# Hybrid decoder block: the retention norm on GpSimd and ScalarE, and four more gate blocks by seven products

## The chip, the cores and the metric

The kernel runs on one core of one Trainium2 chip. The metric is the device time of one execution in microseconds (us), taken as the median of several runs. PE is TensorE (matmuls), PEld its weight loads, DVE is VectorE, ACT is ScalarE, POOL is GpSimd, and SP is the engine that issues most DMAs.

## The reference, cut to what matters

One layer, batch 1, 1024 positions, width 1024, all float32. The part that the change touches is the retention branch of the token mixer, its gate, and the modulation vector:

```python
mod = jax.nn.silu(c) @ w_ada[l] + b_ada[l]            # 6 x 1024: sh1, sc1, g1, sh2, sc2, g2
h = modulate(rms_norm(x, norm1_g[l]), sh1, sc1)
rq, rk, rv, rg = parts[0], parts[1], parts[2], parts[3]   # parts of h @ w_in
ro = retention(rq, rk, heads(rv, RET_HEADS))          # 4 heads, dk 256, dv 512, chunks of 128
mu = jnp.mean(ro, axis=-1, keepdims=True)
var = jnp.mean(jnp.square(ro - mu), axis=-1, keepdims=True)
ro = (ro - mu) * lax.rsqrt(var + GN_EPS)
ro = ro * gn_g + gn_b
ret_out = (jax.nn.silu(rg) * ro) @ w_ret_out
```

In a chunk: `s = (q k^T) * decay`, `o = s v + (q state) * q_decay`, `state = state * decay^128 + (k * k_decay)^T v`. The rest of the block (dilated window attention, merge by gates, squared-ReLU MLP, norms) is not touched.

## The kernel before

**Precision.** Every float32 matmul is made of three passes: each operand is split into a high part (a copy in the reduced matmul format) and a low part (the rest), and `mm3` adds low x high, high x low and high x high (lines 207, 209, 211). A weight split (`split_w`) is a ScalarE copy (line 197) and a VectorE subtraction (line 198).

**Direct blocks and pairs.** A block is 128 output columns for all 1024 positions. A direct block (`proj_mm`) takes 8 k tiles x 3 passes x 2 halves of 512 positions = 48 matmuls. Two blocks can instead be made together as a pair by a seven-product scheme for 2 x 2 block matrices (class `Blocks`): 7 products x 4 k tiles x 3 passes = 84 matmuls, with sums of weight quarters and of results on VectorE beside them. A pair of kind "s" holds Silu gate blocks of retention; its result goes to DRAM (`srg_d`) and comes back in the head that needs it.

**Stages and their times in the profile.** The first values and operand sums; 22 pairs (`queries_keys`, 180 to 597 us); the values of retention (`values`, 597 to 712 us, ten groups of four); retention (712 to 981 us, `chunk`, 4 heads x 8 chunks); then attention, merge and MLP.

**Modulation rows.** From the 17th pair on `mod_turn` is called after every product of a pair and after every value group's part. It loads one row of `w_ada` (512 KB) with SP into one of two buffers (`cs`, shown as cossin), and two rows later the buffer is used by a VectorE multiply-accumulate (line 1252) before it is loaded again (line 1254). 32 rows are taken so.

**A retention chunk.** The order is written out by hand, and every engine issues in that order. In chunk (h, c), with g = 8 h + c: two `kv` products (state update); some units of the gate (`rg_mm(n)`, one unit is one k tile, six matmuls); the VectorE state update (line 745), its ScalarE high part (749) and VectorE low part (750); `ahead(2)`, which splits the weights of the next step; `s_kt(g + 1)`, which makes the scores sT and the transposed key kT of the next chunk, and from them `sm`, `smh`, `sml`, `kh`, `kl`; the output `o`; `jit_qk` for two chunks ahead (ScalarE copy, GpSimd low part, line 617); the transposes oT of the last chunk's normed output with their ScalarE copies; one more gate unit; the norm. The norm is bn_stats, bn_aggr and a small step on VectorE (772 to 774), a power on GpSimd (775), a small product (776) and the 512-wide `onm` (778) on VectorE. In the first four chunks of heads 1 to 3 `u_final` follows for the head before: a ScalarE scale and shift (688), the VectorE product with the gate (690), and the DMA of `y`.

**Gate units.** Each head has four gate blocks: three are direct, 8 units each, and three units stand in each chunk (`RG`); the fourth comes from a pair.

**PSUM.** PSUM has eight banks. During retention four are one-bank tiles with tag "s" (sT, kT, kv, o, oT in rotation) and four are two two-bank tiles with tag "mm" (the gate).

Of the kernel before, what the change touches and what calls it, by code (L numbers as in the profile page):

```python
# [40 lines left out]
CS_QD = 132  # L41
CS_QD2 = 136
# [98 lines left out]
def block_kernel(ctx, tc, io, stop=None, dbg=None):  # L141
# [12 lines left out]
    def banks(single):  # L154
# [11 lines left out]
    def ps_mm(name):  # L166
        return PS["p"].tile([P, 2, 512], F32, tag="mm", bufs=2, name=name)

# [343 lines left out]
    def etile(name, dt=F32):  # L512
        return R["p"].tile([P, 1024], dt, tag="E", bufs=12, name=name)
# [116 lines left out]
    def s_kt(i):  # L630

        p = R["p"]
        g = i
        h, c = divmod(g, NC)
        t = hd["j", g]
        ps = ps_s(f"sT{h}{c}")
        for i in range(2):
            nc.tensor.matmul(ps[:, :2 * C], t[:, 0, 2 + i, :], t[:, :, i, :], start=i == 0, stop=False,
                             skip_group_check=True)
            nc.tensor.matmul(ps[:, :C], t[:, 1, 2 + i, :], t[:, 0, i, :], start=False, stop=i == 1,  # L640
                             skip_group_check=True)
        pk = ps_s(f"kT{h}{c}", (P, 2, P)) if c < NC - 1 else None
        if pk is not None:
            for i in range(2):
                nc.tensor.transpose(pk[:, i, :], hd["qk", g][:, 2 + i], ident)
# [7 lines left out]
        nc.vector.tensor_add(sm, sm, ps[:, C:2 * C])  # L653
        nc.vector.tensor_mul(sm, sm, decay[:, h * C:(h + 1) * C])
        hd["s", g] = (smh, sml)
        if pk is not None:
            kd = ct[:, CS_KDEC + h:CS_KDEC + h + 1]
            if g == 0:
                kh, kl = R["kh"], R["kl"]
            else:  # L660
                kh = p.tile([P, 2, P], F32R, tag="kh", bufs=1, name=f"kh{h}{c}")
                kl = p.tile([P, 2, P], F32R, tag="kl", bufs=1, name=f"kl{h}{c}")
            nc.scalar.mul(kh, pk, kd)
        nc.scalar.copy(smh, sm)
        if pk is not None:
            nc.vector.scalar_tensor_tensor(flat(kl), flat(pk), kd, fv(flat(kh)), op0=ALU.mult, op1=ALU.subtract)
            hd["k", g] = (kh, kl)
        nc.vector.tensor_sub(sml, sm, fv(smh))

    def on_T(h, c):  # L670

        po = ps_s(f"oT{h}{c}", (P, 4, P))
        on = hd["o", h, c]
        if c == 0:
            hd["on", h] = [etile(f"on{h}{e}") for e in range(4)]
        for e in range(4):
            nc.tensor.transpose(po[:, e, :], on[:, e * P:(e + 1) * P], ident)
        for e in range(4):
            nc.scalar.copy(hd["on", h][e][:, c * C:(c + 1) * C], po[:, e, :])

    def u_final(h, es=range(4), queue=nc.sync):
        for e in es:
            i = h * 4 + e
            t = hd["on", h][e]
            for hf in range(2):
                neg = 16 if hf == i % 2 else 0
                b = t[:, 512 * hf:512 * hf + 512]
                nc.scalar.activation(b, b, AF.Identity, scale=gnv[0][:, neg + i:neg + i + 1],
                                     bias=gnv[1][:, neg + i:neg + i + 1])
            nc.vector.tensor_mul(t, t, hd["srg", h, e])  # L690
            queue.dma_start(y_d[h][:, 2 * (i % 2):2 * (i % 2) + 2, e // 2], t.rearrange("p (t x) -> p t x", t=2))
# [12 lines left out]

    def rg_out(h, c):

        if "rgs" in hd:
            e = {1: 0, 2: 0, 4: 1, 5: 1, 7: 2}[c]
            hd["srg", h, e] = etile(f"srg{h}{e}")
            nc.scalar.activation(hd["srg", h, e], flat(hd.pop("rgs")), AF.Silu)  # L710
        if c == 6:
            hd["srg", h, 3] = etile(f"srg{h}3")
            nc.sync.dma_start(hd["srg", h, 3], srg_d[h])

    def chunk(h, c, ahead, w=None):
# [21 lines left out]
        rg_mm(1 if g == 0 else RG[h][c] - 1)  # L737
# [9 lines left out]
        if g > 0:  # L747
            for i in range(len(kvs)):
                nc.scalar.copy(sh1[:, i, :], st[:, i, :])  # L749
                nc.vector.tensor_sub(sl1[:, i, :], st[:, i, :], fv(sh1[:, i, :]))  # L750
        if g == 0:
            jit_qk(2)
        ahead(2)
        if 0 < g < NG - 1:
            s_kt(g + 1)
# [15 lines left out]
        gr = p.tile([P, 1], F32, tag="gr", bufs=2, name=f"gr{h}{c}")  # L771
        nc.vector.bn_stats(bn, po)
        nc.vector.bn_aggr(ba, bn)
        nc.vector.tensor_scalar(gr, ba[:, 1:2], ct[:, CS_QD2 + h:CS_QD2 + h + 1], GN_EPS, op0=ALU.mult, op1=ALU.add)
        nc.gpsimd.tensor_tensor(gr, gr, mhalf[:, 0:1], op=ALU.pow)
        nc.vector.tensor_mul(gr, gr, ct[:, CS_QD + h:CS_QD + h + 1])
        on = p.tile([P, DV], F32, tag="on", bufs=1, name=f"onm{h}{c}")
        nc.vector.tensor_scalar(on, po, ba[:, 0:1], gr, op0=ALU.subtract, op1=ALU.mult)
        hd["o", h, c] = on
        rg_out(h, c)  # L780
        if h > 0 and c < 4:
            u_final(h - 1, (c,))
# [8 lines left out]
    srg_d = [dram.tile([P, S], F32, name=f"srgd{h}") for h in range(H)]  # L791
# [333 lines left out]
    def sums_of_h(name, ms=range(4)):  # L1125

        for m in ms:
# [18 lines left out]
            if name != "t4":  # L1146
# [10 lines left out]
    s_pairs = [("s", i) for i in range(H // 2)]  # L1157
    PAIRS = [{"r": r_pairs, "a": a_pairs, "g": g_pairs, "k": k_pairs, "s": s_pairs}[i].pop(0)
             for i in "rargrarkrargrarkgagass"]
# [29 lines left out]
    def a_out(q, n, x, y=None):  # L1189
# [19 lines left out]
        if n in ("12", "21"):  # L1209
# [6 lines left out]
            elif pair[0] == "s":  # L1216
                dst = srg_d[2 * pair[1] + i]
# [166 lines left out]
    def values(ahead):  # L1384
# [43 lines left out]
        banks(False)  # L1428
# [4 lines left out]

    for h in range(H):
        for c in range(NC):
            steps.add((lambda h, c: lambda ahead, *w: chunk(h, c, ahead, *w))(h, c),
                      ([wsplit(io["w_rg"][3 * h + (0, 2, 5).index(c)])] if c in (0, 2, 5) else []),
# [393 lines left out]
    def att_step(pair, a):  # L1831

        def body(*args):
            ps = ps_mm(f"ak{pair}1{a}")
# [993 lines left out]
def _constants():  # L2828
# [9 lines left out]
    for h in range(H):  # L2838
# [4 lines left out]
        cst[:, CS_QD + h] = np.exp(lg * (i + 1))  # L2843
        cst[:, CS_QD2 + h] = np.exp(2 * lg * (i + 1))
# [19 lines left out]
def pack(x, c, w_ada, b_ada, norm1_g, w_in, rel_bias, ret_gn_g, ret_gn_b,  # L2864
# [17 lines left out]
        "w_rg": _cols(w[:, 4096:6144].reshape(1024, 4, 4, P)[:, :, :3].reshape(1024, 1536)),  # L2882
        "w_rg2": _pairs(w[:, 4096:6144].reshape(1024, 4, 4, P)[:, :, 3].reshape(1024, 512)),
# [33 lines left out]
```

## Time and profile before

| | |
|---|---|
| median of 3 runs | 2175.4 us (2174.5 to 2175.61) |
| profiled execution | 2173.28 us, its span 2171.3 us |
| TensorE | 2144.7 us busy (99%), 10036 matmuls, clock 0.999 |
| VectorE | 1520.4 us busy (70%) |
| ScalarE | 959.3 us busy (44%) |
| GpSimd | 165.7 us busy (8%) |
| HBM | 324.13 MB read, 160.32 MB written |

Matmuls overlap, so the time of one in the profile (0.39 us for 512 columns) is longer than the distance from one to the next. The end of an instruction on VectorE and ScalarE overlaps a little with the start of the next one, too; distances between starts tell what a step costs its engine.

### The profile page before, as it was taken

The numbers are of one execution on the slowest core, as the hardware profiler recorded it, in microseconds if no ns is written. First come the engines' busy times: TensorE is split into PE (matmuls) and PEld (weight loads), VectorE is DVE, ScalarE is ACT, GpSimd is POOL, SyncE is SP. The second block draws the span as 40 slices with busy tenths as digits, with TensorE's granted clock in tenths as the row PEclk, the third lists the DMA queues.
The fourth block names the chain that finished last, engine by engine and source line by source line (L and its number), as shares of the span: only waits on it lengthen the run. The fifth ranks groups of instructions, "written<-read, shape, count | busy, mean of one in ns | idle before, by whom it ended". The sixth has DMA issues, their size and how long they took to land. (4 is left out here: it accounts for less than half of the span.)

```text
span 2171.3 us, 27289 instructions
## 1 busy us (share of the span) xinstructions
PE 2144.7 (99%) x10036; PEld 1782.4 (82%) x10036; DVE 1520.4 (70%) x2358; ACT 959.3 (44%) x1757; POOL 165.7 (8%) x199
## 2 busy tenths in 40 slices
PE   8999999999999999999999999999999999999998
PEld 6888888888887788888888888888778888888887
DVE  6886777777656677776667644677876665877855
ACT  5543322323334455556656625434454455533413
POOL 0001111100001112211110000001000000000003
PEclk9999999999999999999999999999999999999999
DMA  9859998835588744436877366653144435645322
GB/s 383 282 208 309 285 306 265 243 117 194 186 301 303 234 148 151 160 127 197 218 194 196 115 245 211 217 191 132 64 175 160 150 136 193 253 135 173 109 88 78
DMA packets 162674, 425.18 MB, mean 196 GB/s; under 512 B 28005, under 2 KB 55916, under 8 KB 159468
## 3 DMA queue, kind: packets, MB, share of 16 engines
q1 hardware_dynamic: 150264, 374.90, 48.3%
q0 software_dynamic: 9584, 48.24, 9.9%
q8 instruction: 79, 1.29, 0.2%
q10 hardware_dynamic: 2692, 0.30, 0.1%
q14 instruction: 55, 0.45, 0.1%
HBM read 324.13 MB, written 160.32 MB: 223 GB/s over the span
## 5 line engine op out<-in xcount | busy, mean ns | idle before, releaser
L207 PE MATMUL qap<-hh,qaw 128*128 128x512 f32 x264 | 102.7, 389 | 0.0
L209 PE MATMUL qap<-hl,qaw 128*128 128x512 f32 x264 | 102.7, 389 | 0.0
L211 PE MATMUL qap<-hh,qaw 128*128 128x512 f32 x264 | 102.7, 389 | 0.0
L617 POOL TENSOR_TENSOR j<-qk,j 128x512 fp32r<-128x512 f32 x32 | 42.8, 1338 | 454.8 <-ACT j L616 454.8
L2235 POOL TENSOR_TENSOR accnf<-accnf,sqnf 128x256 f32<-128x256 f32 (+1 forms) x18 | 16.6, 922 | 609.6 <-ACT sqnf L2231 609.6
L2339 ACT ACTIVATE a<-a 128x512 f32<-128x512 f32 x48 | 30.3, 631 | 72.8 <-DVE a L2338 71.3
L749 ACT CAST stateh<-state 128x512 fp32r<-128x512 f32 x54 | 32.9, 622 | 57.8 <-DVE state L745 55.7
L209 PEld LDWEIGHTS qap<-hl,qaw 128*128 128x128 f32 x264 | 49.5, 188 | 10.4
L211 PEld LDWEIGHTS qap<-hh,qaw 128*128 128x128 f32 x264 | 49.6, 188 | 10.3
L207 PEld LDWEIGHTS qap<-hh,qaw 128*128 128x128 f32 x264 | 49.5, 188 | 10.2
L2547 ACT CAST w2h<-w2s 128x512 fp32r<-128x512 f32 x36 | 22.4, 621 | 80.3 <-DVE w2s L2585 80.3
L264 DVE TENSOR_TENSOR fw<-w1r,fw 128x512 fp32r<-128x512 f32 x48 | 32.9, 688 | 33.6 <-ACT fw L254 33.6
L264 DVE TENSOR_TENSOR qaw<-wa,qaw 128x512 fp32r<-128x512 f32 x66 | 44.0, 687 | 9.4 <-ACT qaw L254 9.4
L2070 DVE TENSOR_TENSOR rwl<-rwl,rwh 128x1024 fp32r<-128x1024 f32 x25 | 30.2, 1221 | 29.0 <-ACT rwh L2100 29.0
L207 PE MATMUL fp<-h2h,fw 128*128 128x512 f32 x128 | 50.0, 390 | 0.0
L209 PE MATMUL fp<-h2l,fw 128*128 128x512 f32 x128 | 49.8, 389 | 0.0
L211 PE MATMUL fp<-h2h,fw 128*128 128x512 f32 x128 | 49.8, 389 | 0.0
L207 PE MATMUL roa<-rh,rwl 128*128 128x512 f32 x128 | 49.8, 389 | 0.0
L209 PE MATMUL roa<-rl,rwh 128*128 128x512 f32 x128 | 49.8, 389 | 0.0
L211 PE MATMUL roa<-rh,rwh 128*128 128x512 f32 x128 | 49.8, 389 | 0.0
L1603 ACT ACTIVATE P<-P,ng 128x128 f32<-128x128 f32 (+1 forms) x96 | 41.9, 438 | 17.6 <-DVE ng L1595 17.5
L292 DVE TENSOR_TENSOR qat<-qat,qap 128x512 f32<-128x512 f32 x22 | 15.1, 688 | 42.8 <-PE qap L211 35.8
(3089 smaller groups left out, 7187.8 us busy)
## 6 DMA issues: line engine op xcount, KB each, us to landing
cossin<-in_w_ada_dram SPq DMA_DIRECT2D x32, 512.0 KB, 3.5
v<-vd SPq DMA_DIRECT2D x32, 512.0 KB, 4.3
w1r<-in_w_ff_dram SPq DMA_DIRECT2D x32, 512.0 KB, 4.6
yt<-y POOLq DMA_DIRECT2D x24, 512.0 KB, 7.5
xsd<-as SPq DMA_DIRECT2D x24, 512.0 KB, 3.1
w2r<-in_w_ff2s_dram SPq DMA_DIRECT2D x24, 512.0 KB, 6.4
em<-in_w_ada_dram SPq DMA_DIRECT2D x16, 512.0 KB, 10.2
wrvs<-in_w_rv_dram POOLq DMA_DIRECT2D x16, 512.0 KB, 9.8
```

What stands on the lines that cost most here:

```text
L207: nc.tensor.matmul(o, wl, xh, start=first, stop=False, skip_group_check=skip)
L209: nc.tensor.matmul(o, wh, xl, start=False, stop=False, skip_group_check=skip)
L211: nc.tensor.matmul(o, wh, xh, start=False, stop=last, skip_group_check=skip)
L264: nc.vector.tensor_sub(t[:, 512:], src, fv(t[:, :512]))
L292: nc.vector.tensor_sub(u, u, b)
L617: nc.gpsimd.tensor_sub(t[:, 1], src, fv(t[:, 0]))
L749: nc.scalar.copy(sh1[:, i, :], st[:, i, :])
L1603: nc.scalar.activation(v, v, AF.Exp, bias=ng[:, blk:blk + 1], accum_out=st[:, g, blk, 2 + a:3 + a])
L2070: nc.vector.tensor_sub(lo, fv(lo), fv(hi))
L2235: (nc.vector if f == 7 else nc.gpsimd).tensor_add(G["acc", key], G["acc", key], sq)
L2339: nc.scalar.activation(o, o, AF.Relu)
L2547: nc.scalar.copy(hi, src)
```

## The change

- The norm: the small step on VectorE becomes one addition, with the epsilon scaled for each position (`CS_EQ`). GpSimd makes minus the mean (a product with -1), the power, and their product. The 512-wide norm is a ScalarE activation with scale and bias from these, and leaves VectorE.
- The gate: two blocks of each head are direct, two come from pairs; there are four "s" pairs instead of two, 24 pairs in all. `RG` has 64 units instead of 96, spread unevenly. The Silu of a direct block is made in two halves.
- PSUM in retention: five one-bank tiles "s" and three one-bank tiles "rg". The banks change back at the first attention step.
- Weights of a gate block are tied to the step before the one that uses them. `ahead(2)` stands behind `s_kt`, and so does the second low part of the state (in the middle of `s_kt`'s VectorE steps).
- `u_final`: its ScalarE part stands ahead of the norm's activation, its product and DMA in the next chunk.
- Copies of oT: two of 256 columns instead of four of 128.
- Modulation rows: one in two turns instead of 7 in 16.

```diff
-CS_QD = 132
-CS_QD2 = 136
+CS_NEG = 132
+CS_EQ = 136
...
-        PS["n"] = 8 if single else 4
+        PS["n"] = 8 if single else 5 if ret else 4
...
+    def ps_rg(name):
+        return PS["p"].tile([P, 512], F32, tag="rg", bufs=3, name=name)
...
-        return R["p"].tile([P, 1024], dt, tag="E", bufs=12, name=name)
+        return R["p"].tile([P, 1024], dt, tag="E", bufs=4, name=name)
...
-    def s_kt(i):
+    def s_kt(i, mid=None):
...
             hd["k", g] = (kh, kl)
+        if mid:
+            mid()
         nc.vector.tensor_sub(sml, sm, fv(smh))
...
-        for e in range(4):
-            nc.scalar.copy(hd["on", h][e][:, c * C:(c + 1) * C], po[:, e, :])
+        for e in range(2):
+            nc.scalar.copy(hd["on2", h][e][:, :, c * C:(c + 1) * C], po[:, 2 * e:2 * e + 2, :])
...
-    RG = ((6, 2, 2, 3, 3, 3, 3, 2),) + ((3,) * NC,) * (H - 1)
+    RG = (6, 2, 2, 2, 1, 1, 2, 3), (2, 2, 2, 2, 2, 1, 1, 3), (2, 2, 2, 2, 2, 1, 1, 3), (3, 2, 2, 2, 2, 2, 2, 0)
...
-                hd["rgk"], hd["rgw"], hd["rgp"] = 0, hd["rgws"].pop(0), ps_mm("rg")
+                hd["rgk"], hd["rgw"], hd["rgp"] = 0, hd["rgws"].pop(0), [ps_rg(f"rg{i}") for i in range(2)]
...
-                hd["rgs"] = hd["rgp"]
+                i = hd["rgi"] = hd.get("rgi", -1) + 1
+                t = hd["srg", i // 2, i % 2] = etile(f"srg{i // 2}{i % 2}")
+                for j, ps in enumerate(hd["rgp"]):
+                    nc.scalar.activation(t[:, 512 * j:512 * j + 512], ps, AF.Silu)
...
-        rg_mm(1 if g == 0 else RG[h][c] - 1)
+        rg_mm(1 if g == 0 else max(RG[h][c] - 1, 0))
...
-        if g > 0:
-            for i in range(len(kvs)):
+        def low(i):
+            nc.vector.tensor_sub(sl1[:, i, :], st[:, i, :], fv(sh1[:, i, :]))
+
+        if g > 0 and kvs:
+            for i in range(2):
                 nc.scalar.copy(sh1[:, i, :], st[:, i, :])
-                nc.vector.tensor_sub(sl1[:, i, :], st[:, i, :], fv(sh1[:, i, :]))
+            low(0)
         if g == 0:
             jit_qk(2)
-        ahead(2)
+            ahead(2)
         if 0 < g < NG - 1:
-            s_kt(g + 1)
+            s_kt(g + 1, (lambda: low(1)) if kvs else None)
+        if g > 0:
+            ahead(2)
+        if "um" in hd:
+            hd.pop("um")()
...
-        rg_mm(0 if g == 0 else 1)
+        rg_mm(min(RG[h][c], 1) if g > 0 else 0)
...
-        nc.vector.tensor_scalar(gr, ba[:, 1:2], ct[:, CS_QD2 + h:CS_QD2 + h + 1], GN_EPS, op0=ALU.mult, op1=ALU.add)
-        nc.gpsimd.tensor_tensor(gr, gr, mhalf[:, 0:1], op=ALU.pow)
-        nc.vector.tensor_mul(gr, gr, ct[:, CS_QD + h:CS_QD + h + 1])
+        nc.vector.tensor_scalar_add(gr[:, 0:1], ba[:, 1:2], ct[:, CS_EQ + h:CS_EQ + h + 1])
+        nc.gpsimd.tensor_tensor(gr[:, 2:3], ba[:, 0:1], ct[:, CS_NEG:CS_NEG + 1], op=ALU.mult)
+        nc.gpsimd.tensor_tensor(gr[:, 1:2], gr[:, 0:1], mhalf[:, 0:1], op=ALU.pow)
+        nc.gpsimd.tensor_tensor(gr[:, 2:3], gr[:, 1:2], gr[:, 2:3], op=ALU.mult)
+        if h > 0 and c < 4:
+            hd["um"] = u_final(h - 1, (c,), late=True)
         on = p.tile([P, DV], F32, tag="on", bufs=1, name=f"onm{h}{c}")
-        nc.vector.tensor_scalar(on, po, ba[:, 0:1], gr, op0=ALU.subtract, op1=ALU.mult)
+        nc.scalar.activation(on, po, AF.Identity, scale=gr[:, 1:2], bias=gr[:, 2:3])
         hd["o", h, c] = on
         rg_out(h, c)
-        if h > 0 and c < 4:
-            u_final(h - 1, (c,))
...
-             for i in "rargrarkrargrarkgagass"]
+             for i in "rargrarkrargrarkgagassss"]
...
-        while turn["i"] < NV + 2 and 7 * turn["n"] > 16 * turn["i"]:
+        while turn["i"] < NV + 2 and turn["n"] > 2 * turn["i"]:
...
+    RGW, n = [], 0
+    for g in range(NG):
+        RGW += [g - (g > 2)] * (n < 8 * len(RGW) + 1 <= n + RG[g // NC][g % NC])
+        n += RG[g // NC][g % NC]
...
+            if pair == a == 0:
+                banks(False)
...
-        cst[:, CS_QD + h] = np.exp(lg * (i + 1))
-        cst[:, CS_QD2 + h] = np.exp(2 * lg * (i + 1))
+        cst[:, CS_NEG] = -1.0
+        cst[:, CS_EQ + h] = GN_EPS * np.exp(-2 * lg * (i + 1))
```

More of the change, by code (lines that the diff above doesn't have):

```diff
@@ L152, in block_kernel, with banks @@
     PS = {}
-    def banks(single):
+    def banks(single, ret=False):
         if PS:
@@ L674, in on_T, with u_final @@
         if c == 0:
-            hd["on", h] = [etile(f"on{h}{e}") for e in range(4)]
+            hd["on2", h] = [R["p"].tile([P, 2, 1024], F32, tag="EO", bufs=4, name=f"on{h}{e}") for e in range(2)]
+            hd["on", h] = [hd["on2", h][e // 2][:, e % 2] for e in range(4)]
         for e in range(4):
             nc.tensor.transpose(po[:, e, :], on[:, e * P:(e + 1) * P], ident)
-        for e in range(4):
-            nc.scalar.copy(hd["on", h][e][:, c * C:(c + 1) * C], po[:, e, :])
-    def u_final(h, es=range(4), queue=nc.sync):
+        for e in range(2):
+            nc.scalar.copy(hd["on2", h][e][:, :, c * C:(c + 1) * C], po[:, 2 * e:2 * e + 2, :])
+    def u_final(h, es=range(4), queue=nc.sync, late=False):
         for e in es:
@@ L790, in block_kernel @@
     ak_d = {(p, a): dram.tile([P, S], F32, name=f"akd{p}{a}") for p in range(2) for a in range(2)}
-    srg_d = [dram.tile([P, S], F32, name=f"srgd{h}") for h in range(H)]
+    srg_d = {(h, i): dram.tile([P, S], F32, name=f"srgd{h}{i}") for h in range(H) for i in range(2)}
     h12_d = [dram.tile([P, 2, 512], F32, name=f"h12d{m}") for m in range(4)]
@@ L1216, in a_out @@
             elif pair[0] == "s":
[L1217 removed]
+                dst = srg_d[pair[1], i]
             else:
```

29 lines of the change are left out of this document (15 added, 14 removed).

## The prediction, made before the changed kernel had run

> **What bounds the kernel now.** I read the page first: TensorE is busy nearly all of the span.
>
> ```profile
> span 2171.3 us, 27289 instructions
> ...
> PE 2144.7 (99%) x10036; PEld 1782.4 (82%) x10036; DVE 1520.4 (70%) x2358; ACT 959.3 (44%) x1757; POOL 165.7 (8%) x199
> ```
>
> Only 26.6 us of the span are without a matmul, so a gain must come from fewer matmuls or from those 26.6 us. Next the busy time by stage (columns: length, then PE, PEld, DVE, ACT, POOL busy, granted clock, DMA share, GB/s): pairs, values, and two stretches of retention.
>
> ```profile
> 400.00:500.00 100.00, 100.00 (x442) 82.78 (x442) 75.35 (x118) 28.22 (x50) 6.81 (x10) 1.00 0.56 168
> ...
> 640.00:660.00 20.00, 18.08 (x79) 14.32 (x78) 11.26 (x17) 4.97 (x7) 0.00 (x0) 1.00 0.95 385
> ...
> 760.00:800.00 40.00, 40.00 (x202) 33.46 (x201) 28.45 (x63) 21.42 (x54) 9.00 (x10) 1.00 0.42 140
> 800.00:840.00 40.00, 39.94 (x200) 33.25 (x199) 32.02 (x65) 21.54 (x53) 7.73 (x9) 1.00 0.52 172
> ```
>
> The pair stage is saturated: 442 matmuls in 100 us, one each 0.226 us (their own 0.39 us overlap). Retention is saturated too, at granted clock 1.00, but VectorE is busy 32.02 of 40 us beside it. The values stage has holes. The waits from 597 to 735 us (total, times, longest) say where:
>
> ```profile
> ACT vo L1362 <- DMA vd<-vo: 10.6, 3, 4.7
> ...
> PE vc L209 <- DVE vwl L1328: 1.9, 2, 1.5
> ...
> PE rg L207 <- DVE vr L1367: 1.1, 1, 1.1
> ...
> PE kv L207 <- ACT state L763: 0.9, 1, 0.9
> ```
>
> The last row shows how PSUM banks go round. With four "s" banks, the first kv of chunk 1 takes the bank of the second kv of chunk 0, whose last reader is the ScalarE copy to `state`; that is what it waits for. Banks are thus given out in strict rotation, and a tile waits for the last reader of the tile as many places back as there are banks.
>
> Then one retention chunk in order of time, TensorE first (start, length, line):
>
> ```profile
> 658.15 0.50 PE L209 MATMUL vc<-vwl,xat 128*128 128x512 f32 x1 [1.46 <-DVE vwl L1328]
> ...
> 804.79 0.60 PE L677 MATMUL oT<-ct,onm 128*128 128x128 f32 x4
> 805.15 0.71 PE L207 MATMUL rg<-hh,raw_5684l 128*128 128x512 f32 x2
> ...
> 806.62 0.39 PE L207 MATMUL kv<-v,kl 128*128 128x512 f32 x1
> ...
> 807.99 0.61 PE L207 MATMUL rg<-hh,raw_5684l 128*128 128x512 f32 x2
> ...
> 810.71 0.28 PE L638 MATMUL sT<-j 128*128 128x256 f32 x1
> ...
> 811.11 0.40 PE L645 MATMUL kT<-ct,qk 128*128 128x128 f32 x2
> 811.27 0.48 PE L207 MATMUL o<-stateh,j 128*128 128x512 f32 x1
> ...
> 813.44 0.60 PE L677 MATMUL oT<-ct,onm 128*128 128x128 f32 x4
> ...
> 815.27 0.39 PE L207 MATMUL kv<-v,kl 128*128 128x512 f32 x1
> ```
>
> From kv to kv is 8.65 us. Two gate units (a unit is one k tile: three passes on two halves, six matmuls) take 810.71 - 807.99 = 2.72, so 1.36 each; kv takes 1.37, sT 0.40, oT with one unit 806.62 - 804.79 = 1.83. The first row, from the values stage, shows a matmul after a wait: 0.50 long instead of 0.39, so a restart costs about 0.1.
>
> VectorE, ScalarE and GpSimd in the same chunk, and one weight split later:
>
> ```profile
> 800.01 0.81 DVE L778 TENSOR_SCALAR onm<-o,ba,gr 128x512 f32<-128x512 f32 x1
> 800.74 1.22 DVE L690 TENSOR_TENSOR on<-on,srg 128x1024 f32<-128x1024 f32 x1
> 801.87 1.28 DVE L745 SCALAR_TENSOR_TENSOR state<-state,kv 128x512 f32<-128x512 f32 x2
> 803.24 1.29 DVE L750 TENSOR_TENSOR statel<-state,stateh 128x512 fp32r<-128x512 f32 x2
> 804.45 0.28 DVE L653 TENSOR_TENSOR sm<-sm,sT 128x128 f32<-128x128 f32 x1
> ...
> 805.63 0.69 DVE L772 BATCH_NORM_STATS2 bn<-o 128x6 f32<-128x512 f32 x1
> ...
> 806.58 0.21 DVE L774 TENSOR_SCALAR gr<-ba,ct 128x1 f32<-128x1 f32 x1
> 807.82 0.16 DVE L776 TENSOR_TENSOR gr<-gr,ct 128x1 f32<-128x1 f32 x1 [1.02 <-POOL gr L775]
> 808.08 0.81 DVE L778 TENSOR_SCALAR onm<-o,ba,gr 128x512 f32<-128x512 f32 x1
> ...
> 821.09 1.23 DVE L198 TENSOR_TENSOR raw_5955l<-raw,raw_5955h 128x1024 fp32r<-128x1024 f32 x1 [0.25 <-ACT raw_5955h L197]
> ```
> ```profile
> 802.59 1.22 ACT L749 CAST stateh<-state 128x512 fp32r<-128x512 f32 x2 [2.67 <-DVE state L745]
> ```
> ```profile
> 807.23 0.55 POOL L775 TENSOR_TENSOR gr<-gr,ct 128x1 f32<-128x1 f32 x1
> ```
>
> VectorE's round is 808.08 - 800.01 = 8.07 of the 8.65 us, and 1.02 of it is the wait for the power on GpSimd. So before, TensorE sets the pace with 0.6 us to spare.
>
> **The sum.** The profiled execution took 2173.28 us (span 2171.3 and 2.0 around it); the median of the runs is 2175.4. I add differences to the median. About 0.2% (4.35 us) is what a measurement here can tell from no change.
>
> *Matmuls.* Four gate blocks (4 x 8 = 32 units) leave retention: 32 x 1.36 = 43.5 us. They return as two pairs of seven products, 7 x 4 x 3 = 84 matmuls a pair: 2 x 84 x 0.226 = 37.9 us. Net -5.6 us. The pairs' extra sums, splits and Silu lie beside saturated matmuls in a stage where VectorE has a quarter free (75.35 of 100); the four more 512 KB stores and loads on SP's queue lie in stretches whose DMA share is 0.56 and 0.42. I cost both at nothing.
>
> *Modulation rows.* They go from 7 rows in 16 turns to one in 2, and begin at the same place, with 14 more turns of pairs before the values. Before: 38 turns in pairs, so 34 rows last to turn 76, nearly the end of the values (40 turns). After: 52 turns in pairs, the last row at turn 67, the 15th of the values. Each row is a 512 KB load on SP's queue, which stops there until VectorE has used the buffer:
>
> ```profile
> SPq L1254 <- DVE cossin L1252: 36.7, 12, 9.0
> ```
>
> In the second half of the values neither this stop nor the load competes any more with the weight loads and `vd` stores (DMA share 0.95 at 640:660). The waits of 1.9, 1.1 and 0.9 us lie there or just behind. Bounds: +1 (the faster rate disturbs the first values) and -3.9 (all go). I take -2.5.
>
> *The norm.* VectorE loses the 512-wide `onm` (0.73 to the next start), the last `gr` product and the wait, about 2.0 a chunk: its round falls to 6.1 with a `y` product (1.13) and 4.9 without. TensorE's chunk falls to 8.65 - 1.36 = 7.29 with two units and 5.93 with one. VectorE alone keeps up. But `onm` is now at the end of a chain bn, GpSimd three times, ScalarE, and ScalarE works in order: behind it stand the next chunk's state casts. With five "s" banks, kT of chunk g+2 takes the bank of o of chunk g, whose last reader is that ScalarE instruction. So TensorE waits if this loop is longer than its chunk. What its new steps cost, from the nearest groups (busy, mean ns):
>
> ```profile
> L2235 POOL TENSOR_TENSOR accn<-accn,sqn 128x512 f32<-128x512 f32 x12 | 15.5, 1295 | 324.0 <-ACT sqn L2231 324.0
> ...
> L2235 POOL TENSOR_TENSOR accnf<-accnf,sqnf 128x256 f32<-128x256 f32 x12 | 8.9, 738 | 15.4 <-ACT sqnf L2231 15.4
> ```
> ```profile
> L688 ACT ACTIVATE on<-on,gnt 128x512 f32<-128x512 f32 x32 | 24.3, 833 | 0.0
> ...
> L710 ACT ACTIVATE srg<-rg 128x1024 f32<-128x1024 f32 x12 | 12.6, 1050 | 3.1 <-PE rg L211 3.1
> ...
> L906 ACT ACTIVATE avo<-av,n1rs 128x512 f32<-128x512 f32 x8 | 5.0, 690 | 0.3 <-issue 0.3
> ```
>
> A GpSimd product falls by 557 ns for 256 columns, so at one column about 0.19 is left; the upper bound is the power's 0.55. I take 0.2, since the slope is of the same operation. The ScalarE norm reads PSUM with two pointers: between 0.69 (one pointer, PSUM) and 0.83 (two, SBUF); I take 0.79.
>
> The loop: from the state casts to bn 805.63 - 802.59 = 3.04, plus 0.4 because a state low part (0.6) now stands behind `kl`; the `y` product 1.13; bn to the end of the third small step 806.79 - 805.63 = 1.16; the power and the second product with their hand-over 0.6 + 0.25; the norm with its hand-overs 0.85. Together 7.4, without the `y` product 6.3; a weight split (1.14) in the chunk comes on top.
>
> - Chunks 1 to 4 of heads 1 to 3: 7.4 against 7.29, and a first chunk of the head that is 1.4 us shorter because it has no state product (six of the nine matmuls between 811.27 and 813.44). About 0.7 a head: 2.
> - Chunks 5 and 6 of heads 1 and 2 have one unit: 6.3, in the chunk with a split 7.4, against 5.93, plus the lag brought along: 2.3 a head, 4.6. Head 0 has no `y` products and comes without lag; head 3 keeps two units.
> - The gate's own banks are now three single ones. Where a block starts right behind the last one (chunk 7 of heads 0 and 1, which have no kv between), it waits for the first half's Silu (half of 1.05, and its place in ScalarE's queue): 0.7 and 1.0.
>
> Sum 8.3, and about twelve restarts of 0.1: +9.5 us. Bounds: 0 (lag soaked up by chunk 7, which has no kv and three units) and, with GpSimd products at 0.55, 0.7 more for every loop: about +17.
>
> Total: -5.6 - 2.5 + 9.5 = +1.4, so 2176.8 us.
>
> **Rivals.**
> *The loop keeps up.* If GpSimd's products come at 0.1 or the norm of ScalarE hides under TensorE's units, stalls fall to 1 to 3: -5.6 - 2.5 + 2 = -6.1, 2169.3. For it: 7.4 against 7.29 is a tie, and VectorE gets a quarter of its time back. Against: one-unit chunks are 0.4 short even without lag.
> *The norm becomes the bound (slower).* GpSimd's products at 0.55: loop 8.1 against 7.29, TensorE waits at kT in nearly every chunk of heads 1 to 3, 17 us: -5.6 - 2.5 + 17 = +8.9, 2184.3. It turns slower by 0.2% when the stalls pass 12.5 us, which a product of about 0.35 gives. For it: GpSimd's power at one column took 0.55, so a fixed share can be large. Against: the slope of the two product rows. The Trainium skill (Perfetto Trace Analysis, Optimization Strategy) says that a gap which repeats on the engine that should be saturated can mean too few SBUF or PSUM buffers; the wait of kv for `state` is such a case here, once.
> *The rows bring nothing.* The relief is 0 and the stalls are as forecast: +3.9, 2179.3, still within 0.2%.
> *The pairs stall.* That the seven products save nothing would need idle matmuls in the added pairs; the pair stage shows 100.00 of 100, so I leave it 3 in 100, among the slower.
>
> **How the numbers follow.** Forecast with its neighbours, rows included: 0.45. Loop keeps up: 0.23. Norm bound, or stalls above 12.5 for another reason: 0.32. The likeliest case's own range is 2172 to 2179.7. For 8 in 10 I reach to both other cases: 2168 to 2185.5. Faster by over 0.2% is below 2171.05: 0.23; slower is above 2179.75: 0.32; the rest 0.45.
>
> **What would show it.** The pair stage ends near 635 us with no new waits; from there to the first rg the matmul waits shrink from over 3 us to about 1. Retention (712 to 981) is 43.5 minus the stalls shorter: about 34. The waits of TensorE name kT on the ScalarE `onm` for most of the new idle time, and rg on `srg` twice. Wrong would be: no wait on `onm` at all (then the loop keeps up), GpSimd's `gr` products well over 0.3, a stall in the added pairs, or new idle time behind retention.

## The result, and the profile after

| | median (us) | runs | ratio to before, 95% interval |
|---|---|---|---|
| before | 2174.95 | 6 | 1 |
| after | 2185.01 | 6 | 1.0048 [1.0035, 1.0061] |

The change costs 10.06 us. The predicted 2176.8 was 8.2 us too low; the range (to 2185.5) holds the result, but the likeliest case, no difference that can be measured, did not come.

The page of the changed kernel, span and busy time:

```profile
span 2184.9 us, 27334 instructions
...
PE 2146.3 (98%) x10012; PEld 1783.3 (82%) x10012; DVE 1519.9 (70%) x2322; ACT 981.2 (45%) x1749; POOL 182.1 (8%) x263
```

TensorE has 24 matmuls fewer and no less busy time, and the span has 38.6 us without a matmul (26.6 before). Where they lie is read from the first start of one tile for each stage: `vc` opens the values, `rg` the retention, `ak` what follows. The rows are groups by tile (min/median/max ns; first and last start). Before, then after:

```profile
L207 PE MATMUL vc<-vwh,xat x32: 387/389/396, 598.6 to 666.9; 128*128 128x512 f32 x32
...
L207 PE MATMUL rg<-hh,raw_5355l x16: 389/393/497, 712.4 to 731.8; 128*128 128x512 f32 x16
...
L207 PE MATMUL ak<-hh,raw_7655l x16: 389/389/481, 980.8 to 991.0; 128*128 128x512 f32 x16
```
```profile
L210 PE MATMUL vc<-vwh,xat x32: 388/389/397, 637.3 to 703.9; 128*128 128x512 f32 x32
...
L210 PE MATMUL rg<-hh,raw_5630l x16: 389/390/478, 748.1 to 765.8; 128*128 128x512 f32 x16
...
L210 PE MATMUL ak<-hh,raw_7280l x16: 388/389/499, 994.5 to 1004.9; 128*128 128x512 f32 x16
```

| us | before | after | difference | predicted |
|---|---|---|---|---|
| up to the values | 598.6 | 637.3 | +38.7 | +37.9 |
| values | 113.8 | 110.8 | -3.0 | -2.5 |
| retention | 268.4 | 246.4 | -22.0 | -34.0 |
| behind it (to the end of the span) | 1190.5 | 1190.4 | -0.1 | 0 |

Two of the three terms came out. The miss lies in retention, 12.0 us. (These are the two profiled executions. They lie 13.6 us apart where the medians differ by 10.06: the changed kernel's is the slowest of its six. So up to 3.5 us of the 12.0 may belong to the execution and not to the kernel.) Retention should have lasted 268.4 - 43.5 = 224.9 us without stalls and lasted 21.5 more; I had allowed 9.5. The waits of the changed kernel, 0 to 1100 us (total, times, longest):

```profile
PE o L210 <- ACT onm L800: 8.6, 5, 3.1
PE o L210 <- DVE state L757: 3.4, 7, 0.7
...
PE rg L210 <- ACT srg L718: 2.0, 2, 1.8
```

The first two rows are the new ones: 12.0 us in which TensorE waits for the norm on ScalarE or for VectorE's state update. The new steps of the norm are not to blame; their groups (busy, mean ns) read as forecast, 0.2 and 0.79:

```profile
L796 POOL TENSOR_TENSOR gr<-gr 128x1 f32<-128x1 f32 x32 | 6.2, 193 | 2.5
L794 POOL TENSOR_TENSOR gr<-ba,ct 128x1 f32<-128x1 f32 x32 | 6.0, 189 | 35.5 <-DVE ba L792 35.4
...
L800 ACT ACTIVATE onm<-o,gr 128x512 f32<-128x512 f32 x32 | 24.9, 779 | 60.5 <-POOL gr L796 60.4
```

What changed its duration is an instruction that the change only moves, the `y` product (VectorE's product of normed output and gate in `u_final`). The group before, then after:

```profile
L690 DVE TENSOR_TENSOR on<-on,srg 128x1024 f32<-128x1024 f32 x16 | 19.5, 1220 | 5.6 <-ACT on L688 5.4
```
```profile
L698 DVE TENSOR_TENSOR on<-on,srg 128x1024 f32<-128x1024 f32 x16 | 32.7, 2044 | 3.8 <-ACT on L694 3.8
```

Twelve of the sixteen lie in retention and take 2.29 to 2.32 us; the last four, behind it, 1.22. In order of time in one chunk, VectorE (the `y` product and bn_stats, called bn below) and then GpSimd:

```profile
821.05 2.32 DVE L698 TENSOR_TENSOR on<-on,srg 128x1024 f32<-128x1024 f32 x1
823.29 0.68 DVE L791 BATCH_NORM_STATS2 bn<-o 128x6 f32<-128x512 f32 x1
```
```profile
820.87 1.42 POOL L620 TENSOR_TENSOR j<-qk,j 128x512 fp32r<-128x512 f32 x1 [3.58 <-ACT j L619]
```

GpSimd's low part of `j` starts 0.18 us ahead and ends at 822.29. From there to 823.37, where the `y` product ends, are 1.08 us, about its own time. It reads as if VectorE had stood still until GpSimd was done. Before, the `y` product stood behind the norm, at 800.74, with GpSimd idle, and `j` came at about 806. The loop of a chunk follows; the first bn of three chunks in a row:

```profile
894.43 0.69 DVE L791 BATCH_NORM_STATS2 bn<-o 128x6 f32<-128x512 f32 x1
...
902.62 0.69 DVE L791 BATCH_NORM_STATS2 bn<-o 128x6 f32<-128x512 f32 x1
...
910.81 0.69 DVE L791 BATCH_NORM_STATS2 bn<-o 128x6 f32<-128x512 f32 x1
```

The period is 8.19 us, where TensorE's own chunk was forecast at 7.29. TensorE stops a little in each chunk, where `o` waits for the state, and for long where it waits for the norm of the chunk before. The row of ScalarE behind it shows that norm for the chunk at 904.56:

```profile
904.56 0.50 PE L210 MATMUL o<-stateh,j 128*128 128x512 f32 x1 [0.65 <-DVE state L757]
...
913.85 0.80 PE L210 MATMUL o<-stateh,j 128*128 128x512 f32 x1 [3.09 <-ACT onm L800]
915.30 0.63 PE L210 MATMUL o<-stateh,j 128*128 128x512 f32 x1
```
```profile
904.84 0.78 ACT L800 ACTIVATE onm<-o,gr 128x512 f32<-128x512 f32 x1 [2.76 <-POOL gr L796]
```

At 904.56 `o` started before the norm of the chunk before had begun; at 913.85 it waited for it. From the one to the other are 9.29 us, 1.10 more than the period. The chunk at 913.85 also has one gate unit instead of two, so less work to cover the wait (one unit is 1.36 us). The two other long stops, 1.73 at 843.70 and 2.10 at 977.88, stand in chunks with two units.

The last two rows of TensorE show a second cost: behind the long stop matmuls last 0.63 us instead of 0.39. The windows (length, PE, PEld, DVE, ACT, POOL, granted clock, DMA share, GB/s) show the clock behind two of the stops:

```profile
840.00:850.00 10.00, 8.27 (x35) 6.61 (x34) 8.49 (x16) 4.01 (x10) 2.33 (x5) 0.83 0.41 137
...
910.00:920.00 10.00, 6.91 (x24) 5.47 (x24) 7.77 (x16) 4.76 (x10) 3.38 (x6) 0.66 0.61 191
```

0.17 and 0.34 of 10 us are 1.7 and 3.4 us of full rate lost. With a third such place (970 to 990, at 0.89 and 0.94: 1.7) that makes 6.8 us, and with the waits (8.6 + 3.4 + 2.0) 20.8 of the 21.5.

### The profile page after: what moved, and what is told of

The parts are those of the page before. It is cut to its first block, busy times and chain, and to the rows that moved or that the text cites. A ratio compares the mean times of both kernels' runs of the same rounds, so it can differ in the third digit from the quotient of the medians.

```text
span 2184.9 us, 27334 instructions
## 1 busy us (share of the span) xinstructions
PE 2146.3 (98%) x10012; PEld 1783.3 (82%) x10012; DVE 1519.9 (70%) x2322; ACT 981.2 (45%) x1749; POOL 182.1 (8%) x263
## 3 DMA queue, kind: packets, MB, share of 16 engines
q8 instruction: 79, 1.29, 0.2%
## 5 line engine op out<-in xcount | busy, mean ns | idle before, releaser
L210 PE MATMUL qap<-hh,qaw 128*128 128x512 f32 x288 | 112.1, 389 | 0.0
L214 PE MATMUL qap<-hh,qaw 128*128 128x512 f32 x288 | 112.1, 389 | 0.0
L212 PE MATMUL qap<-hl,qaw 128*128 128x512 f32 x288 | 112.1, 389 | 0.0
L210 PEld LDWEIGHTS qap<-hh,qaw 128*128 128x128 f32 x288 | 54.1, 188 | 11.3
L214 PEld LDWEIGHTS qap<-hh,qaw 128*128 128x128 f32 x288 | 54.1, 188 | 11.2
L212 PEld LDWEIGHTS qap<-hl,qaw 128*128 128x128 f32 x288 | 54.1, 188 | 11.2
L800 ACT ACTIVATE onm<-o,gr 128x512 f32<-128x512 f32 x32 | 24.9, 779 | 60.5 <-POOL gr L796 60.4
L760 DVE TENSOR_TENSOR statel<-state,stateh 128x512 fp32r<-128x512 f32 x54 | 37.1, 686 | 21.1 <-ACT stateh L764 21.1
```

The costliest lines, as they stand in the source:

```text
L210: nc.tensor.matmul(o, wl, xh, start=first, stop=False, skip_group_check=skip)
L212: nc.tensor.matmul(o, wh, xl, start=False, stop=False, skip_group_check=skip)
L214: nc.tensor.matmul(o, wh, xh, start=False, stop=last, skip_group_check=skip)
L800: nc.scalar.activation(on, po, AF.Identity, scale=gr[:, 1:2], bias=gr[:, 2:3])
```

## Experiments

Theory 1: GpSimd holds up the `y` product, and that makes the loop too long; the clock comes on top. Theory 2: the loop is too long without that, as the prediction had it. Theory 3: a PSUM bank comes free too late. Theory 4: the `y` product is slow because of where its buffers lie. Times are medians, and ratios are to runs of the kernel before in the same series (2174.7 to 2175.4); the changed kernel's 2185.01 is from the series above (before: 2174.95).

**The y product behind the state updates.**

```
             for i in range(2):
                 nc.scalar.copy(sh1[:, i, :], st[:, i, :])
+            if "um" in hd:
+                hd.pop("um")()
             low(0)
...
-        if "um" in hd:
-            hd.pop("um")()
         po = ps_s(f"o{h}{c}")
```

> The changed kernel with one thing moved: the late y product of VectorE stands behind the two state updates of the chunk (where VectorE waits for the ScalarE state casts) instead of ahead of bn_stats (where it ran beside GpSimd's low part of j). Same arithmetic. Theory 1 (the y product is doubled by GpSimd beside it, 1.22 to 2.32, and stands in the norm's loop): the twelve y products in retention fall to 1.2 to 1.3, the loop of the chunks with a y product falls below 7.3, the matmul waits for onm and state together fall from 12.0 us to under 5, the granted clock stays at 1.00 in most of retention, and the time falls by 8 to 18 us against the changed kernel, to 2167 to 2177. Theory 2 (the loop is too long in itself, mostly in the one-unit chunks): the y products get short but the waits for onm stay above 8 us and the time falls by less than 5 us. Theory 4 (the doubling comes from where the buffers lie): the y products stay at 2.3 in the new place.

Measured: 2167.85 us, ratio to before 0.9964 [0.995, 0.9978]; 17.2 below the changed kernel. Group, waits (590 to 1100 us), and VectorE over a chunk:

```profile
L698 DVE TENSOR_TENSOR on<-on,srg 128x1024 f32<-128x1024 f32 x16 | 19.5, 1222 | 4.3 <-ACT on L694 4.3
```
```profile
PE rg L210 <- ACT srg L718: 2.0, 2, 1.8
PE va L210 <- ACT va L1396: 1.8, 1, 1.8
PE ak L210 <- DVE raw_7282l L201: 1.3, 1, 1.3
```
```profile
822.89 0.69 DVE L791 BATCH_NORM_STATS2 bn<-o 128x6 f32<-128x512 f32 x1
...
825.65 1.22 DVE L698 TENSOR_TENSOR on<-on,srg 128x1024 f32<-128x1024 f32 x1
827.76 0.69 DVE L760 TENSOR_TENSOR statel<-state,stateh 128x512 fp32r<-128x512 f32 x1 [0.89 <-ACT stateh L764]
...
830.18 0.69 DVE L791 BATCH_NORM_STATS2 bn<-o 128x6 f32<-128x512 f32 x1
```

The same sixteen products, the same buffers, 1.22 us each. They lie where VectorE waits for ScalarE's state casts anyway (0.89 is still left), no wait for `onm` or `state` remains, and the period of the loop is TensorE's 7.29. Retention (749.9 to 975.6) lasts 225.7 us, against 224.9 without stalls. Theories 2 and 4 fall. This edit alone does not tell the standstill from the product's mere place in the loop; the next ones do.

**Low part of j on VectorE**, nothing else.

```
-        nc.gpsimd.tensor_sub(t[:, 1], src, fv(t[:, 0]))
+        nc.vector.tensor_sub(t[:, 1], src, fv(t[:, 0]))
```

> The changed kernel, its y product in its place ahead of bn_stats, but the low part of j (128x512, two inputs in SBUF) on VectorE behind it instead of on GpSimd beside it. Same arithmetic. If the two engines shut each other out: nothing is left on GpSimd that could hold the y product, so it falls from 2.32 to 1.22; the low part costs VectorE 0.6 in every chunk instead, so the loop of a chunk with a y product falls by about 0.5 (8.19 to 7.7, against 7.29), and waits for onm and state fall from 12.0 to 5 to 10 us; time 2174 to 2183. If the y product is long for another reason (its place in the chunk, its buffers): it stays at 2.3, the loop grows by 0.6, and the time rises to 2190 or more.

Measured: 2181.89 us, 1.0033 [1.002, 1.0046], at the upper end of what I expected. Group and waits:

```profile
L698 DVE TENSOR_TENSOR on<-on,srg 128x1024 f32<-128x1024 f32 x16 | 19.5, 1219 | 3.9 <-ACT on L694 3.9
```
```profile
PE o L210 <- DVE state L757: 3.4, 6, 0.9
PE rg L210 <- ACT srg L718: 3.4, 2, 3.2
PE sT L641 <- DVE j L620: 1.7, 4, 0.5
...
PE o L210 <- ACT onm L800: 0.7, 2, 0.4
```

In its old place, with GpSimd idle, the `y` product takes 1.22. So GpSimd beside it made the 2.32, not the place. Waits for `onm` and `state` fall from 12.0 to 4.1 (5 to 10 expected). But VectorE now has the low part in the same loop (0.6 a chunk): three bn in a row start at 898.72, 906.41 and 914.10, so the loop is 7.69, still above 7.29. And a wait of 3.17 us for `srg` lowers the clock (0.84 and 0.82 from 860 to 880, 3.4 us). So the time stays 14 us above the first experiment's.

**Who waits for whom: two further places of the y product.** First in the kernel before, between bn_stats and bn_aggr:

```
         nc.vector.bn_stats(bn, po)
+        if h > 0 and c < 4:
+            u_final(h - 1, (c,))
         nc.vector.bn_aggr(ba, bn)
...
-        if h > 0 and c < 4:
-            u_final(h - 1, (c,))
```

> The kernel before with one thing moved: the y product (with its scale on ScalarE) stands between bn_stats and bn_aggr of a chunk, so that it begins while GpSimd works on the low part of j. Same arithmetic. It measures the disputed cost by itself. Theory 1: the twelve y products in retention go from 1.22 to 1.8 to 2.4, GpSimd's low part of j from 1.34 to 1.4 to 1.9 in those chunks, and the four y products behind retention stay at 1.2. Theory 4 (placement of the buffers in the changed kernel): both stay as they were, 1.2 and 1.3. The time goes up in either case, since the norm now waits for the y product: by some 5 to 25 us.

Measured: 2187.79 us, 1.0064 [1.0047, 1.0082], both durations unchanged (1.22 and 1.34). It does not tell the theories apart: the scale on ScalarE, queued behind the `j` cast, held the product until `j` was over (it ran 809.29 to 810.51, `j` 807.25 to 808.55). So the scale had to come a chunk earlier, and the product ahead of bn_stats, still in the kernel before (with `u_final` split in two as in the changed kernel):

```
...
+        if "um" in hd:
+            hd.pop("um")()
         po = ps_s(f"o{h}{c}")
...
+        if h > 0 and c < 4:
+            hd["um"] = u_final(h - 1, (c,), late=True)
         on = p.tile([P, DV], F32, tag="on", bufs=1, name=f"onm{h}{c}")
...
-        if h > 0 and c < 4:
-            u_final(h - 1, (c,))
```

> The kernel before with the y product (scaled on ScalarE in the chunk before) just ahead of bn_stats, so that it begins a little ahead of GpSimd's low part of j. Same arithmetic. The earlier attempt put it behind bn_stats, where it began only after j was done. If the two engines shut each other out: the y product, first to start, stays at 1.2, and GpSimd's low part of j takes 1.8 to 2.4 us instead of 1.29 in those twelve chunks (or the reverse where j starts first: y at 1.8 to 2.4). If they share in proportion: both grow to 1.5 to 1.9. If placement of the buffers was the cause in the changed kernel: both stay. The time is 0 to 10 us above the kernel before.

Measured: 2174.28 us, 1.0001 [0.9992, 1.001]. VectorE, then GpSimd:

```profile
797.05 1.22 DVE L692 TENSOR_TENSOR on<-on,srg 128x1024 f32<-128x1024 f32 x1
```
```profile
797.41 2.01 POOL L617 TENSOR_TENSOR j<-qk,j 128x512 fp32r<-128x512 f32 x1 [6.62 <-ACT j L616]
805.36 1.77 POOL L617 TENSOR_TENSOR j<-qk,j 128x512 fp32r<-128x512 f32 x1 [5.39 <-ACT j L616]
```

Now VectorE starts first and keeps its 1.22; GpSimd ends at 799.42, 1.15 after the end of the `y` product at 798.27. In the next chunk the product ran from 804.76 to 805.98, and GpSimd started later behind it, lasted 1.77 and ended at 807.13, again 1.15 after the product. In all twelve chunks it is so within 0.01 (GpSimd's step lasts 2.01, 1.77 or 1.54, alone 1.29): GpSimd's end follows the product's end and not its own start. Sharing would have made both longer. The first to start runs at full speed, the other stands still until its end, apart from about 0.14 us of its own work (1.29 - 1.15, and 1.22 - 1.08 above). The time of this kernel does not suffer: TensorE's waits have none for `j`.

Third, the changed kernel with the product right behind the norm's small steps:

```
-        if "um" in hd:
-            hd.pop("um")()
         po = ps_s(f"o{h}{c}")
...
         hd["o", h, c] = on
+        if "um" in hd:
+            hd.pop("um")()
         rg_out(h, c)
```

> The changed kernel with the y product behind VectorE's last small step of the norm, that is beside the small GpSimd steps (128x1) instead of beside the low part of j. Same arithmetic. If VectorE and GpSimd shut each other out while one of them runs an operation with two inputs in SBUF (the later one waits for the earlier one to end, as 2.32 = 1.42 - 0.18 + 1.1 reads in the changed kernel): the y product stays at 1.2, and one of the small GpSimd steps takes 1.2 to 1.7 us instead of 0.19 or 0.55 in the twelve chunks, the ScalarE norm comes 1 us later, and the time stays within 5 us of the changed kernel's 2185. If they share bandwidth in proportion to what each moves: the small steps stay at 0.19 and 0.55, the y product at 1.2 to 1.3, and the time falls to 2168 to 2176.

Measured: 2173.23 us, 0.9991 [0.9981, 1.0]. GpSimd's power and second product as groups, then one power in order of time (the `y` product beside it ran from 815.24 to 816.47):

```profile
L793 POOL TENSOR_TENSOR gr<-gr,ct 128x1 f32<-128x1 f32 x32 | 20.5, 641 | 0.8 <-DVE gr L791 0.3
L794 POOL TENSOR_TENSOR gr<-gr 128x1 f32<-128x1 f32 x32 | 12.1, 377 | 2.5
```
```profile
815.28 1.59 POOL L793 TENSOR_TENSOR gr<-gr,ct 128x1 f32<-128x1 f32 x1
```

Even a one-column GpSimd step stands still. In sum 20.5 - 17.4 + 12.1 - 6.2 = 9.0 us (17.4 and 6.2 in the changed kernel): in ten of the twelve chunks one of the two steps is longer by 0.73 to 1.08, in the two others neither. The mechanism is as expected, my time for it was not: I had put it within 5 us of 2185. A small step loses 0.9 on average where the product had lost 1.1, and TensorE waits 4.1 us for `onm` and none for `state`. Why the time falls as far as it does was not tried further.

**Six banks for the small products, two for the gate blocks.**

```
-        PS["n"] = 8 if single else 5 if ret else 4
+        PS["n"] = 8 if single else 6 if ret else 4
...
-        return PS["p"].tile([P, 512], F32, tag="rg", bufs=3, name=name)
+        return PS["p"].tile([P, 512], F32, tag="rg", bufs=2, name=name)
```

> The changed kernel with six PSUM banks for the small products and two for the gate blocks, instead of five and three. Same arithmetic. Theory 3 (o of chunk g+1 waits because it gets the bank of o of chunk g, whose last reader is the norm): with a sixth bank the matmul waits for onm fall from 8.6 us to under 2; the gate blocks, now with the two banks of one block, wait longer for Silu (1.8 before, 3 to 6 now). Time 0 to 8 us lower than the changed kernel. Theory 1 and 2 (the loop itself, through VectorE and ScalarE in order, is longer than the chunk): the wait only moves to another product of the small banks (oT waits for onm, state product for state), the sum of waits stays within 3 us of the changed kernel and so does the time.

Measured: 2184.04 us, 1.0041 [1.0028, 1.0053]; the changed kernel's 1.0048 lies in this interval. Waits:

```profile
PE sT L641 <- POOL j L620: 3.8, 4, 1.6
PE oT L683 <- ACT onm L800: 3.4, 7, 1.0
PE rg L210 <- ACT srg L718: 2.5, 2, 2.1
PE kv L210 <- DVE kl L669: 2.4, 10, 0.6
```

The bank is no longer waited for, but 9.6 us of waits for `j`, `onm` and `kl` turn up at three other products instead of 12.0. Theory 3 falls: the bank was only where TensorE met the late loop.

**The norm's last step back on VectorE**, with the `y` product behind the state updates.

```
-        nc.gpsimd.tensor_tensor(gr[:, 2:3], ba[:, 0:1], ct[:, CS_NEG:CS_NEG + 1], op=ALU.mult)
...
-        nc.gpsimd.tensor_tensor(gr[:, 2:3], gr[:, 1:2], gr[:, 2:3], op=ALU.mult)
...
-        nc.scalar.activation(on, po, AF.Identity, scale=gr[:, 1:2], bias=gr[:, 2:3])
+        nc.vector.tensor_scalar(on, po, ba[:, 0:1], gr[:, 1:2], op0=ALU.subtract, op1=ALU.mult)
```

> The first experiment's kernel (y product behind the state updates) with the norm's last step back on VectorE: on = (o - mean) * gr in one instruction there, and GpSimd's two products gone. Same arithmetic up to rounding. It shows what moving the norm to ScalarE and GpSimd is worth once the y product is out of the way. VectorE's round in a chunk with a y product is then about 7.6 to 7.9 us (1.28 + 1.22 + 1.3 + 1.0 + 0.3 + 0.7 + 0.4 + 0.7 wait for the power + 0.8) against 7.29 of TensorE. If the move was needed: matmul waits for onm or state of 4 to 12 us come back and the time is 3 to 12 us above the first experiment's 2167.9. If it was not: within 2 us of it.

Measured: 2171.32 us, 0.9981 [0.9972, 0.9989]. By the medians the move to ScalarE is worth 3.5 us, the lower end of what I expected; the intervals of this and the first experiment overlap a little (0.9972 to 0.9978). The waits that came back are smaller than I expected: 1.3 us for `onm`, none for `state`, and 1.8 for `j`.

**The old rate of the modulation rows.**

```
-        while turn["i"] < NV + 2 and turn["n"] > 2 * turn["i"]:
+        while turn["i"] < NV + 2 and 7 * turn["n"] > 16 * turn["i"]:
```

> The changed kernel with the modulation rows at the rate of the kernel before (7 rows in 16 turns instead of 1 in 2). Same arithmetic. If the prediction's step on the rows holds (the rows competed with weight loads and vd stores in the second half of the values): the matmul waits between the start of the values and the first gate block go up again by 1 to 4 us, to about 3 to 5, and the time is 1 to 4 us above the changed kernel. If the rows brought nothing: waits and time stay within 1 us. With 14 more turns ahead of the values the old rate ends the rows by turn 76 of 92, some 16 turns before the end, so a value near the lower end is the more likely.

Measured: 2187.28 us, 1.0051 [1.0038, 1.0064], not to be told from the changed kernel. The values last 111.4 us instead of 110.8 (113.8 before), and among the kernels of this study with the same code up to there they lasted 109.3 to 112.6. So the rate brings nothing that shows; the 3.0 us come with the rest of the change. Which part of it was not tried: with two more pairs ahead the rows end earlier at the old rate too (VectorE's last use at 705.7, where the values end at 749.9; before at 706.2 of 712.4; in the changed kernel at 680.0). Retention, whose code is the same, lasts 243.8 here and 246.4 in the changed kernel's profile, which shows how far two executions differ.

**Other unit counts**, on top of the first experiment: no gate block begins straight behind the end of the last one.

```
-    RG = (6, 2, 2, 2, 1, 1, 2, 3), (2, 2, 2, 2, 2, 1, 1, 3), (2, 2, 2, 2, 2, 1, 1, 3), (3, 2, 2, 2, 2, 2, 2, 0)
+    RG = (6, 2, 2, 2, 2, 2, 1, 2), (2, 2, 2, 2, 2, 1, 1, 2), (3, 2, 2, 2, 2, 1, 1, 2), (3, 2, 2, 2, 2, 2, 3, 0)
```

> The first experiment's kernel with the gate units dealt otherwise over the chunks (RG), so that no block begins straight behind the end of the last one; the same 64 units. Same arithmetic. The matmul wait for srg (2.0 us, 1.8 of it at once) falls to under 0.5, and no other wait grows by over 1 us: 1 to 3 us below 2167.9. If the three gate banks and the weight loads (now a little earlier or later) make new waits instead: within 1 us of it or above.

Measured: 2164.44 us, 0.9955 [0.9943, 0.9968], the fastest kernel here: 10.3 us below before and 20.6 below the changed one. The wait for `srg` is gone from its list, and retention (748.4 to 971.7) lasts 223.3 us, 2.4 less than in the first experiment.

**What a stop does to the clock.** The last kernel with stops put in: a power repeated on GpSimd, ten more times in one chunk, or five more times in each of four chunks.

```
+        for _ in range(10 if g == 19 else 0):
+            nc.gpsimd.tensor_tensor(gr[:, 1:2], gr[:, 0:1], mhalf[:, 0:1], op=ALU.pow)
         nc.gpsimd.tensor_tensor(gr[:, 1:2], gr[:, 0:1], mhalf[:, 0:1], op=ALU.pow)
```

> The kernel with the other gate counts (2164.4, no waits for onm) with one stall put in: in chunk 3 of the third head GpSimd makes the power ten times over instead of once (ten times 0.62 us, same result), so that the norm of that chunk comes 6 us late and TensorE stops for about 4 to 6 us once. If a stop of TensorE lowers the clock behind it: the granted clock falls below 0.9 in the 10 us behind the stall, the matmuls there run one in 0.43 instead of 0.23, and the time rises by the stall and 2 to 4 us more. If the clock dips of the changed kernel have another cause: granted clock 1.00 behind it, and the time rises by the stall alone.

> The kernel with the other gate counts with four shorter stalls: in chunks 1 to 4 of the third head GpSimd makes the power five more times (3.1 us each, same result), so that TensorE stops for 2 to 3 us in each of four chunks, about 8 to 11 us in all. If only a stop above some 3 us lowers the clock: granted clock 1.00, time up by the stalls alone. If shorter stops that follow one another do so as well, as the changed kernel's 1.7 us stop at 843.70 suggests (0.83 in the 10 us behind it): granted clock 0.8 to 0.95 over these 35 us, and 2 to 6 us beyond the stalls.

One stop: 2169.54 us, 5.1 above the kernel without it. The stop and the windows about it:

```profile
896.95 1.11 PE L683 MATMUL oT<-ct,onm 128*128 128x128 f32 x4 [3.02 <-ACT onm L802]
```
```profile
890.00:900.00 10.00, 6.98 (x31) 5.56 (x29) 4.23 (x9) 3.57 (x9) 5.71 (x11) 0.80 0.68 215
900.00:910.00 10.00, 10.00 (x46) 8.31 (x45) 7.11 (x17) 5.53 (x13) 4.12 (x8) 0.86 0.19 55
```

A stop of 3.02 us (shorter than expected) costs 0.20 + 0.14 of 10 us, 3.4 us, more behind it; retention is 6.1 us longer (229.4). Four stops: 2177.1 us, 12.7 above. TensorE stopped for 1.16, 1.63, 4.02 and 1.79 us:

```profile
901.43 0.80 PE L210 MATMUL o<-stateh,j 128*128 128x512 f32 x1 [4.02 <-ACT onm L802]
...
911.84 0.50 PE L210 MATMUL o<-stateh,j 128*128 128x512 f32 x1 [1.79 <-ACT onm L802]
```
```profile
900.00:910.00 10.00, 8.57 (x31) 6.86 (x31) 4.80 (x11) 3.91 (x9) 4.57 (x9) 0.67 0.58 170
910.00:920.00 10.00, 8.21 (x41) 6.75 (x41) 6.65 (x16) 6.27 (x15) 2.97 (x7) 1.00 0.19 55
```

The 4.02 lowered the clock, by the same 3.4 us, the three shorter ones did not, though they followed one another. So a stop of TensorE can lower the clock, and the clock needs no cause of its own here.

## Why the prediction was right or wrong, point by point

- **Matmuls.** Right: the added pairs cost 38.7 against 37.9, without a wait in them, and retention without stalls would have been 43.5 shorter (the first experiment, with 2.0 us of waits left, comes within 0.8 us of that).
- **Rows.** The size was right (-3.0 against -2.5), but the faster rate, which I gave as the reason, brings nothing that shows. That the rows end earlier ahead of the end of the values is so at the old rate too, so whether this helped stays open.
- **VectorE's round.** 8.07 was read as VectorE's own, with 0.6 us to spare. It is one of uneven distances between starts of `onm` (9.55, 8.07, 8.23), so it shows no spare time. What I built on it, that VectorE alone keeps up, held: it still waits 1.05 us for the state casts in a chunk of the changed kernel (844.18).
- **GpSimd's products and the norm on ScalarE.** Right: 0.19 and 0.78 against 0.2 and 0.79.
- **The loop.** This is the step that failed. It counted "the `y` product 1.13" from a row in which GpSimd was idle. The change puts that product next to GpSimd's low part of `j`, and there it cost 2.24 (from its start to that of bn). I had asked what each engine does in its own order, but not what runs beside a moved instruction on the other engines. With 1.1 more the loop would be 8.5 in place of 7.4; 8.19 was measured, where TensorE has 7.29. The term for chunks 1 to 4, put at 2.0, and the 4.6 for the one-unit chunks, which get the lag from there, were mis-sized by this: 12.0 us of waits for `onm` and `state` were measured in their place. The one-unit chunks are no trouble by themselves: with the `y` product elsewhere and the same counts, no wait for `onm` is left.
- **Restarts.** I took 0.1 for each. The stops were long enough to lower the clock, and 6.8 us went there, which no term held.
- **Banks.** "Given out in strict rotation" was wrong: the wait stands at `o`, not `kT`. In five chunks `o` got the bank of the last chunk's `o`; in others it did not, since it started before that chunk's norm was done (904.56). So which bank it gets is not the same in each chunk. It changed nothing that shows in the time (six banks).
- **Gate block starts.** 1.7 forecast, 2.0 measured, and gone with other counts.
- **The rivals.** The slower one (0.32, with other causes of long stalls) gave 2184.3, near the result, but by a price that did not come: the GpSimd products would have had to take 0.55 (0.35 to be slower by 0.2%), and took 0.19. Its core, that the norm's loop becomes longer than TensorE's chunk in heads 1 to 3, is what happened, in the chunks with a `y` product. The range reached to 2185.5 because of that rival, so it was luck that it holds 2185.01: the cost in it was another one. That the loop keeps up was 0.23, and is what happens once the `y` product is moved: 2167.85, where I had 2169.3.

The Trainium skill (SBUF — State Buffer, Who interferes with whom) states that a VectorE instruction with two inputs in SBUF and a GpSimd instruction that reads SBUF share a port pair, and that whichever starts first holds it for its whole length. The rows at 821.05, 797.41 and 815.28 agree with that; the prediction had not weighed it.

## What to carry to other kernels

When a step is moved, look at what the other engines run at its new place, not only at its own engine's queue: here one two-input product on VectorE lost 1.1 us each time because GpSimd had started a product 0.18 us earlier, and that was enough to make a loop the bound. Put such a product where its engine waits for a third engine anyway; that turned 10 us lost into 7.5 gained. And price a stop of the saturated engine with its clock: here the one stop of 3.02 us that was put in cost 5.1 us by the medians and 6.1 in the profile.

## What the runs showed of the hardware

- VectorE and GpSimd shut each other out in products with both inputs in SBUF, in either direction, even where GpSimd's has one column (0.55 became 1.59). bn_stats, which reads PSUM, ran beside the low part of `j` without loss (0.69, as elsewhere).
- The loss of clock comes in two sizes, 1.7 and 3.4 us of full rate by the windows, and the length of the stop alone does not say which. Stops of 3.02, 3.09 and 4.02 us, and one of 3.17 in the kernel with the low part on VectorE, lost 3.4 each, but one of 3.08 in the kernel with the old rate of the rows lost 1.7 (0.83 from 910 to 920, 1.00 behind it). Stops of 1.73 and 2.10 us (changed kernel), 1.83 (first experiment) and 2.07 (six banks) lost 1.7 each; others of 1.16, 1.63, 1.79, 1.82 and even 2.08 (old rate of the rows, 978.64) lost nothing. The Trainium skill (TensorE: Matmul & The Clock Gate, What's actually happening) gives half rate after an idle window of about 3.4 us that runs freely, without regard to the program. By an estimate from that figure, half rate over one or two such windows would be 1.7 or 3.4 us, which agrees with the two sizes. But stops of 1.73 to 2.10 us, shorter than a window, lost clock here, which that rule does not give, and the measurement decides. What decides between the sizes was not tried.
